# Reordering the seven weight operands in a piece of the down projection

## The chip, the cores and the metric

The kernel runs on one core of one Trainium2 chip. The metric is the device time of one launch in microseconds, the median of several runs. The core has a matrix engine (TensorE; the profile calls its matmuls PE and its weight loads PEld), a vector engine (DVE), a scalar engine (ACT), GpSimd (POOL, here used only to issue transfers) and SyncE (SP, the other issuer of transfers).

## The reference

One layer of a hybrid streaming encoder is run for 384 tokens: 256 frames of a new stream and 8 running streams of 16 frames. A mixer (causal pooling, and a Mamba-2 scan) comes first, then the part in which the change lies:

```python
x = x + rmsnorm(m, p['g_mix_post'])
hdn = jnp.square(jax.nn.relu(rmsnorm(x, p['g_mlp_pre']) @ p['w_up'])) @ p['w_down']
x = x + rmsnorm(hdn, p['g_mlp_post'])
```

w_up is 2048 x 8192, w_down 8192 x 2048, all in float32. The change touches only the order of the work in the product with w_down.

## The kernel before

**Split operands.** Every float32 product is made from two rounded parts of each operand, a high part h and the rest l, and three matmuls: h·h, h·l and l·h. For a weight tile of 128 x 1024 ACT writes the high part (wh) and DVE, when ACT is done, the rest (wl = w - wh). Both come from a pool of three buffers each (wpool, bufs=3), handed out in turn, so the split of one weight half can begin only when TensorE has done its last matmul with the half three before it. All weight halves of the program use these three buffers.

**The MLP stage.** The 384 tokens are three blocks of 128. `up(f)` computes 128 hidden columns: two weight halves with 24 matmuls of 384 columns each. `combine(p)` forms from two of those the left operands of the down projection: blocks of the hidden tile themselves (H11, H31, H22, H12, H32, H3) and sums of them (S1 to S4), by five DVE instructions, two ACT instructions and two DVE subtractions for the rests. After eight `up` calls a chunk c of 1024 hidden rows is ready, four pairs p = 0 to 3, and two pieces follow, `blocks(c, 0)` and `blocks(c, 1)`, with four `up` calls of the next chunk after each. There are 15 pieces; the last quarter of the output for the last chunk is done without them.

**A piece.** `blocks(c, sb)` takes 1024 hidden rows and 1024 output columns. The first two token blocks are multiplied as 2 x 2 blocks with seven products in place of eight (Strassen's scheme in Winograd's form); the third block is multiplied plainly, its sums staying in the PSUM banks A and B over all chunks. Four weight tiles of 128 x 2048 (w11, w12, w21, w22, one buffer each) are fetched over POOL's queue (L1291). From them come seven operands, each split in two halves u = 0, 1 of 1024 columns, the half u serving the pairs p = 2u and 2u+1:

| operand | weight | left operand and PSUM bank | products |
|---|---|---|---|
| a | W11 | H11 into X, H31 into A | 2 |
| b | W21 | H12 into Y, H32 into A | 2 |
| c | W11+W12 | S1 into Y | 1 |
| d | W11+W12+W22 | S2 into X | 1 |
| e | W12+W22 | H31 into B, S3 into X | 2 |
| f | W22 | S4 into Y, H3 into B | 2 |
| g | W21+W11+W12+W22 | H22 into X | 1 |

A product of a half is 2 pairs x 3 matmuls = 6 matmuls of 512 columns. A piece has 11 products, 2 halves of each, so 132 matmuls. X and Y are read out seven times a piece in all by `evict` (L1323): DVE adds or subtracts the bank into the accumulator `acc` in SBUF; in the first chunk ACT copies instead, where the accumulator's block is written for the first time. X and Y keep accumulating after a read-out, so the next matmul into the bank waits until it has been read.

The sums of weights are made by DVE (`add`, L1306, two instructions of 1024 columns each): t1 = w11+w12 and w12 += w22 at the head of the piece, w11 += w12 (L1347), and t1 = w21+w11 (L1355), which overwrites operand c with operand g.

**What sets the order.** TensorE's order is written out: `run` (L1310) holds each group of matmuls behind the one before. For DVE, ACT and POOL the program's order is a priority, not the order of execution: when the program is built, each engine's instructions are put in a row in which an instruction whose inputs are expected to be ready goes ahead of one that stands earlier in the program and is not ready. On the chip each engine then runs its row strictly in order. In the text a piece is told by the time since its first weight load, and `u` (as a unit of time) is the time of six matmuls of 512 columns.

Of the kernel before, what the change touches and what calls it, by code (L numbers as in the profile page):

```python
# [10 lines left out]
ALU = mybir.AluOpType  # L11
# [22 lines left out]
def build(ctx, tc, io):  # L34
# [175 lines left out]
    def in_units(i):  # L210
        return [win[i - 5, 0], win[i - 5, 1]]
# [131 lines left out]
    for b in range(3):  # L343
# [3 lines left out]
            out=dgl[:, b, :], in0=ident, scalar=y1, in1=dgh[:, b, :].bitcast(F32), op0=ALU.mult, op1=ALU.subtract  # L347
# [9 lines left out]
    with tc.tile_pool(name="phc", bufs=1, reuse_waits="tile") as pc, tc.tile_pool(name="phc2", bufs=2, reuse_waits="tile") as pc2:  # L357
# [185 lines left out]
    with tc.tile_pool(name="phd", bufs=2, reuse_waits="tile") as pd, tc.tile_pool(  # L543
        name="phd1", bufs=1, reuse_waits="tile"
# [4 lines left out]
        for i in range(3):  # L549
            b = pd1.tile([P, 24, 19], F32, name=f"cbuf{i}")  # L550
# [292 lines left out]
        for g in range(G + 1):  # L843
# [74 lines left out]
            S1 = D.p[1]  # L918
# [84 lines left out]
    with tc.tile_pool(name="phf", bufs=1, side="right", reuse_waits="tile") as pf, tc.tile_pool(  # L1003
        name="phf2", bufs=2, side="right", reuse_waits="tile"
# [32 lines left out]
        A, L = [], []  # L1037
# [48 lines left out]
        for nb in range(4):  # L1086
# [3 lines left out]
            o = [sstile(f"wo{nb}_{b}") for b in range(3)]  # L1090
# [148 lines left out]
    with ExitStack() as mlp:  # L1239
# [44 lines left out]
        H11, H31, H22, H12, H32, S3, H3, S1, S2, S4 = range(10)  # L1284

        def blocks(c, sb):
            nm = f"{c}_{sb}"
            w = {}
            for i, k in enumerate(("11", "12", "21", "22")):
                w[k] = pr.tile([P, 2048], F32, tag=f"w{k}", name=f"w{k}_{nm}")  # L1290
                gp.dma_start(w[k], io["w_dn"][c, sb, i])  # L1291
            X, Y = (psd.tile([P, 512], F32, tag=n, name=f"{n}{nm}") for n in ("X", "Y"))
            A, B = c3[2 * sb], c3[2 * sb + 1]
            lo_, hi_ = slice(0, 1024), slice(1024, 2048)
            both = (lo_, hi_)
            left, rght = blk(2 * sb), blk(2 * sb + 1)
            C11, C12, C21, C22 = acc[:, 1, left], acc[:, 1, rght], acc[:, 0, left], acc[:, 0, rght]

            def split(t, u, name):
                h = wpool.tile([P, 1024], F32R, tag="wh", name=f"wh_{name}{nm}_{u}")  # L1300
                l = wpool.tile([P, 1024], F32R, tag="wl", name=f"wl_{name}{nm}_{u}")
                s.activation(h, t[:, both[u]], AF.Copy)
                v.tensor_tensor(l, t[:, both[u]], h.bitcast(F32), ALU.subtract)
                return h, l

            def add(out, a, b):  # L1306
                for q in both:
                    v.tensor_tensor(out[:, q], a[:, q], b[:, q], ALU.add)

            def run(hl, seq):  # L1310
                with behind(last[0]):
                    for p, out, j, start in seq:
                        wh, wl = hl
                        h, l, _ = HB[4 * c + p]
                        q = slice(p % 2 * 512, p % 2 * 512 + 512)
                        t = slice(j * P, j * P + P)
                        o, vh, vl = pairs(out), woven(wh[:, q]), woven(wl[:, q])
                        start = start and p == 0
                        te.matmul(o, h[:, t], vh, start=start, stop=False, skip_group_check=True)  # L1319
                        te.matmul(o, h[:, t], vl, start=False, stop=False, skip_group_check=True)  # L1320
                        last[0] = te.matmul(o, l[:, t], vh, start=False, stop=False, skip_group_check=True)  # L1321

            def evict(dst, src, op=ALU.add, first=False):  # L1323
                if first and c == 0:
                    s.activation(dst, src, AF.Copy, scale=-1.0 if op == ALU.subtract else 1.0)
                    return
                v.tensor_tensor(dst, dst, src, op)

            t1 = pr.tile([P, 2048], F32, tag="e", name=f"e{nm}")
            add(t1, w["11"], w["12"])  # L1330
            add(w["12"], w["12"], w["22"])
            a0 = split(w["11"], 0, "a")
            run(a0, [(p, o, j, g) for o, j, g in ((X, H11, True), (A, H31, c == 0)) for p in (0, 1)])
            b0 = split(w["21"], 0, "b")
            run(b0, [(p, o, j, g) for o, j, g in ((Y, H12, True), (A, H32, False)) for p in (0, 1)])
            a1 = split(w["11"], 1, "a")
            b1 = split(w["21"], 1, "b")
            run(a1, [(2, X, H11, False)])
            run(b1, [(2, Y, H12, False)])
            run(a1, [(2, A, H31, False), (3, X, H11, False)])  # L1340
            evict(C11, X, first=True)
            run(b1, [(3, Y, H12, False)])
            evict(C11, Y)
            run(b1, [(2, A, H32, False)])
            run(a1, [(3, A, H31, False)])
            run(b1, [(3, A, H32, False)])
            add(w["11"], w["11"], w["12"])  # L1347

            def simple(t, name, out, j, start):
                for u in (0, 1):  # L1350
                    run(split(t, u, name), [(p, out, j, start) for p in (2 * u, 2 * u + 1)])

            simple(t1, "c", Y, S1, True)
            evict(C22, Y, first=True)
            add(t1, w["21"], w["11"])  # L1355
            simple(w["11"], "d", X, S2, False)
            evict(C12, X, ALU.subtract, first=True)
            e0, e1 = split(w["12"], 0, "e"), split(w["12"], 1, "e")
            run(e0, [(p, B, H31, c == 0) for p in (0, 1)])
            run(e1, [(p, B, H31, False) for p in (2, 3)])  # L1360
            run(e0, [(p, X, S3, False) for p in (0, 1)])
            run(e1, [(p, X, S3, False) for p in (2, 3)])
            evict(C22, X, ALU.subtract)
# [34 lines left out]
        with tc.tile_pool(name="phg", bufs=1, reuse_waits="tile") as pg, tc.tile_pool(  # L1398
            name="phg2", bufs=2, reuse_waits="tile"
# [42 lines left out]
            for nb in (2, 3):  # L1442
                o = [mmtile(f"wd{nb}_{b}") if nb == 2 else psd.tile([P, 512], F32, tag="XY"[b], name=f"wd{nb}_{b}") for b in range(2)]
# [22 lines left out]
                w = []  # L1466
                for kp in range(4):
# [3 lines left out]
                    f_, name = wfetch(io["w_tail"][1, kp], f"wt3_{kp}")  # L1471
# [133 lines left out]
```

## Time and profile before

| | us |
|---|---|
| median of 3 runs | 2651.95 (2651.3 to 2653.32) |
| the profiled execution | 2653.36 |
| its span | 2651.6 |
| PE busy in the span | 2619.0 |
| DVE busy in the span | 1779.1 |
| ACT busy in the span | 1301.5 |

A profiled execution is one run; its own time is 1.76 us above its span and 1.41 us above the median. In the rows below the first column of a timeline is the start in us from the beginning of the span, the second the duration. "[1.54 <-DVE wl_d L1303]" says that the engine stood idle for 1.54 us and that the DVE instruction of line 1303 that writes wl_d ended the wait. A tile's name is followed by its inputs: `X<-wl_d,hh` is a matmul, or its weight load, into the bank X with the rest of operand d.

### The profile page before, as it was taken

What the parts mean: (1) busy time and instruction counts of PE and PEld (TensorE: products, weight loads), DVE (VectorE), ACT (ScalarE), POOL (GpSimd) and SP (SyncE); (2) the same over time, 40 slices, a digit from 0 to 9 for tenths busy, and PEclk for the clock granted to TensorE, in tenths of its full rate; (3) what the DMA queues carried; (4) which work ended last, traced back from release to release, by engine and by line L of the source; (5) the groups of instructions that cost most, each with busy time, mean ns of one, the idle gap of its engine ahead of it and who ended that gap; (6) DMA issues with size and microseconds to landing.
All of it is one profiled execution on the core that took longest, in us unless ns stands there. A gap on an engine that the chain in (4) does not pass through costs nothing.

```text
span 2651.6 us, 40353 instructions
## 1 busy us (share of the span) xinstructions
PE 2619.0 (99%) x15999; PEld 2504.6 (94%) x15999; DVE 1779.1 (67%) x2383; ACT 1301.5 (49%) x1981; POOL 184.2 (7%) x261
## 2 busy tenths in 40 slices
PE   9999999999999999999999999999999999999998
PEld 8999999999999999999999988998989999999997
DVE  6676334788787888766444436667676767767677
ACT  5443235557566666645333335545454444444454
POOL 0000000011110111121000000000000000000000
PEclk9999999999999999999999999999999999999999
DMA  7444446566666676657555554533444444433342
GB/s 273 140 138 153 147 147 206 182 208 209 224 216 212 205 230 212 229 203 245 183 159 159 168 178 163 183 127 135 152 147 139 139 143 139 135 136 135 128 173 105
DMA packets 139421, 457.77 MB, mean 173 GB/s; under 512 B 17568, under 2 KB 44768, under 8 KB 125792
## 3 DMA queue, kind: packets, MB, share of 16 engines
q1 hardware_dynamic: 117552, 330.12, 38.1%
q0 software_dynamic: 21680, 125.07, 12.6%
q8 instruction: 126, 2.06, 0.3%
q14 instruction: 63, 0.52, 0.1%
HBM read 410.26 MB, written 44.86 MB: 172 GB/s over the span
## 4 chain that ended last, share of the span: by engine, by line
PE 92%; DVE 5%; ACT 2%; issue 1%; DMA 0%; DVEq 0%; POOL 0%; ACTq 0%; POOLq 0%
PE pj_up L100 6%; PE pj_up L99 6%; PE pj_up L101 6%; PE pj_x L99 4%; PE pj_x L101 4%; PE pj_x L100 4%; PE pj_z L101 3%; PE pj_z L99 3%; PE pj_sp L100 3%; PE pj_sp L101 3%; PE pj_sp L99 3%; PE pj_z L100 3%; PE X L1320 2%; PE pj_gb L99 2%; PE c L1321 2%; PE c L1319 2%
## 5 line engine op out<-in xcount | busy, mean ns | idle before, releaser
L101 PE MATMUL pj_up<-x1h,wl_up 128*128 128x384 f32 (+1 forms) x1024 | 334.2, 326 | 0.0
L99 PE MATMUL pj_up<-x1h,wh_up 128*128 128x384 f32 (+1 forms) x1024 | 333.9, 326 | 0.0
L100 PE MATMUL pj_up<-x1l,wh_up 128*128 128x384 f32 (+1 forms) x1024 | 333.7, 326 | 0.0
L99 PE MATMUL pj_x<-xgh,wh_x 128*128 128x384 f32 x768 | 252.0, 328 | 0.0
L101 PE MATMUL pj_x<-xgh,wl_x 128*128 128x384 f32 x768 | 250.6, 326 | 0.9 <-DVE wl_x L72 0.9
L100 PE MATMUL pj_x<-xgl,wh_x 128*128 128x384 f32 x768 | 250.4, 326 | 0.0
L71 ACT ACTIVATE wh_up<-w_up 128x1024 fp32r<-128x1024 f32 x126 | 133.0, 1056 | 187.2 <-PE pj_up L100 148.0
L72 DVE TENSOR_TENSOR wl_up<-w_up,wh_up 128x1024 fp32r<-128x1024 f32 x126 | 152.7, 1221 | 100.1 <-ACT wh_up L71 99.0
L101 PEld LDWEIGHTS pj_up<-x1h,wl_up 128*128 128x128 f32 x1024 | 193.5, 189 | 0.9
L100 PEld LDWEIGHTS pj_up<-x1l,wh_up 128*128 128x128 f32 x1024 | 193.5, 189 | 0.4
L99 PEld LDWEIGHTS pj_up<-x1h,wh_up 128*128 128x128 f32 x1024 | 193.5, 189 | 0.4
L99 PE MATMUL pj_sp<-abh,wh_sp 128*128 128x384 f32 x512 | 166.9, 326 | 0.0
L100 PE MATMUL pj_sp<-abl,wh_sp 128*128 128x384 f32 x512 | 166.9, 326 | 0.0
L101 PE MATMUL pj_sp<-abh,wl_sp 128*128 128x384 f32 x512 | 166.9, 326 | 0.0
L101 PE MATMUL pj_z<-xgh,wl_z 128*128 128x384 f32 x512 | 166.9, 326 | 0.0
L100 PE MATMUL pj_z<-xgl,wh_z 128*128 128x384 f32 x512 | 166.9, 326 | 0.0
L99 PE MATMUL pj_z<-xgh,wh_z 128*128 128x384 f32 x512 | 166.9, 326 | 0.0
L72 DVE TENSOR_TENSOR wl_sp<-w_sp,wh_sp 128x1024 fp32r<-128x1024 f32 x64 | 78.3, 1223 | 116.6 <-ACT wh_sp L71 116.6
L71 ACT ACTIVATE wh_x<-w_x 128x1024 fp32r<-128x1024 f32 x96 | 101.0, 1052 | 107.0 <-PE pj_z L100 53.0
L72 DVE TENSOR_TENSOR wl_x<-w_x,wh_x 128x1024 fp32r<-128x1024 f32 x96 | 117.2, 1221 | 52.2 <-ACT wh_x L71 52.2
L71 ACT ACTIVATE wh_sp<-w_sp 128x1024 fp32r<-128x1024 f32 x64 | 67.7, 1058 | 166.4 <-PE pj_sp L100 158.3
L99 PEld LDWEIGHTS pj_x<-xgh,wh_x 128*128 128x128 f32 x768 | 145.1, 189 | 2.6 <-issue 0.4
(449 smaller groups left out, 7122.5 us busy)
## 6 DMA issues: line engine op xcount, KB each, us to landing
w_up<-w_up SPq DMA_DIRECT2D x128, 512.0 KB, 3.5
w<-w_dn POOLq DMA_DIRECT2D x60, 1024.0 KB, 6.7
w_x<-w_in SPq DMA_DIRECT2D x96, 512.0 KB, 3.8
w_z<-w_in SPq DMA_DIRECT2D x64, 512.0 KB, 3.5
w_sp<-w_ssd SPq DMA_DIRECT2D x64, 512.0 KB, 3.5
w_ga<-w_ga SPq DMA_DIRECT2D x32, 512.0 KB, 3.4
w_pp<-w_pp SPq DMA_DIRECT2D x32, 512.0 KB, 3.5
hs<-ssm POOLq DMA_DIRECT2D x16, 1024.0 KB, 6.6
```

Of the source, the lines that this page charges most:

```text
L71: cut[0] = s.activation(h, w, AF.Copy)
L72: cut[1] = v.tensor_tensor(l, w, h.bitcast(F32), ALU.subtract)
L99: te.matmul(out, wh, xh, start=first, stop=False, **how)
L100: te.matmul(out, wh, xl, start=False, stop=False, **how)
L101: return te.matmul(out, wl, xh, start=False, stop=last, **how)
L1319: te.matmul(o, h[:, t], vh, start=start, stop=False, skip_group_check=True)
L1320: te.matmul(o, h[:, t], vl, start=False, stop=False, skip_group_check=True)
L1321: last[0] = te.matmul(o, l[:, t], vh, start=False, stop=False, skip_group_check=True)
```

## The change

The order in a piece before is a and b interleaved, then c, d, e, f, g. After it is a and c interleaved, then f, d, e, b, g, so that operands with two products (a, f, e, b) and with one (c, d, g) alternate. The sum t1 = w21+w11 moves from behind operand c to behind operand e. Operand f is done like e, in the new `double`: both halves are split first, then the first product runs over both halves, then the second; before, f's first half did both products before its second half came. The bank Y holds c and then f's product on top, read out as C22 and C12, and is begun anew for b. The numbers of matmuls, splits, sums, read-outs and transfers are unchanged.

```diff
-            a0 = split(w["11"], 0, "a")
+            def simple(t, name, out, j):
+                for u in (0, 1):
+                    run(split(t, u, name), [(p, out, j, False) for p in (2 * u, 2 * u + 1)])
+
+            def double(t, name, first, second):
+                e = [split(t, u, name) for u in (0, 1)]
+                for out, j, start in (first, second):
+                    for u in (0, 1):
+                        run(e[u], [(p, out, j, start) for p in (2 * u, 2 * u + 1)])
+
+            a0, c0 = split(w["11"], 0, "a"), split(t1, 0, "c")
             run(a0, [(p, o, j, g) for o, j, g in ((X, H11, True), (A, H31, c == 0)) for p in (0, 1)])
-            b0 = split(w["21"], 0, "b")
-            run(b0, [(p, o, j, g) for o, j, g in ((Y, H12, True), (A, H32, False)) for p in (0, 1)])
-            a1 = split(w["11"], 1, "a")
-            b1 = split(w["21"], 1, "b")
-            run(a1, [(2, X, H11, False)])
-            run(b1, [(2, Y, H12, False)])
-            run(a1, [(2, A, H31, False), (3, X, H11, False)])
+            run(c0, [(p, Y, S1, True) for p in (0, 1)])
+            a1, c1 = split(w["11"], 1, "a"), split(t1, 1, "c")
+            run(a1, [(2, X, H11, False), (2, A, H31, False)])
+            run(c1, [(2, Y, S1, False)])
+            run(a1, [(3, X, H11, False), (3, A, H31, False)])
             evict(C11, X, first=True)
-            run(b1, [(3, Y, H12, False)])
+            run(c1, [(3, Y, S1, False)])
+            evict(C22, Y, first=True)
+            add(w["11"], w["11"], w["12"])
+            double(w["22"], "f", (B, H3, c == 0), (Y, S4, False))
+            evict(C12, Y, first=True)
+            simple(w["11"], "d", X, S2)
+            evict(C12, X, ALU.subtract)
+            double(w["12"], "e", (B, H31, False), (X, S3, False))
+            evict(C22, X, ALU.subtract)
+            add(t1, w["21"], w["11"])
+            double(w["21"], "b", (Y, H12, True), (A, H32, False))
             evict(C11, Y)
-            run(b1, [(2, A, H32, False)])
-            run(a1, [(3, A, H31, False)])
-            run(b1, [(3, A, H32, False)])
-            add(w["11"], w["11"], w["12"])
...
-            simple(t1, "c", Y, S1, True)
-            evict(C22, Y, first=True)
-            add(t1, w["21"], w["11"])
-            simple(w["11"], "d", X, S2, False)
-            evict(C12, X, ALU.subtract, first=True)
-            e0, e1 = split(w["12"], 0, "e"), split(w["12"], 1, "e")
-            run(e0, [(p, B, H31, c == 0) for p in (0, 1)])
-            run(e1, [(p, B, H31, False) for p in (2, 3)])
-            run(e0, [(p, X, S3, False) for p in (0, 1)])
-            run(e1, [(p, X, S3, False) for p in (2, 3)])
-            evict(C22, X, ALU.subtract)
-            f0, f1 = split(w["22"], 0, "f"), split(w["22"], 1, "f")
-            run(f0, [(p, o, j, False) for o, j in ((Y, S4), (B, H3)) for p in (0, 1)])
-            run(f1, [(p, o, j, False) for o, j in ((Y, S4), (B, H3)) for p in (2, 3)])
-            evict(C12, Y)
-            simple(t1, "g", X, H22, False)
+            simple(t1, "g", X, H22)
             evict(C21, X, first=True)
```

More of the change, by code (lines that the diff above doesn't have):

```diff
@@ L1341, in blocks @@
-            evict(C11, X, first=True)
-            run(b1, [(3, Y, H12, False)])
-            evict(C11, Y)
-            run(b1, [(2, A, H32, False)])
-            run(a1, [(3, A, H31, False)])
-            run(b1, [(3, A, H32, False)])
-            add(w["11"], w["11"], w["12"])
-            def simple(t, name, out, j, start):
-                for u in (0, 1):
-                    run(split(t, u, name), [(p, out, j, start) for p in (2 * u, 2 * u + 1)])
-            simple(t1, "c", Y, S1, True)
```

## The prediction

> **What bounds the kernel now.** I read the page first, then the waits of TensorE's weight loads, then the busy time of single pieces, then one piece instruction by instruction.
>
> ```profile
> span 2651.6 us, 40353 instructions
> PE 2619.0 (99%) x15999; PEld 2504.6 (94%) x15999; DVE 1779.1 (67%) x2383; ACT 1301.5 (49%) x1981; POOL 184.2 (7%) x261
> ```
>
> TensorE is busy for 99% of the span, so an order of operands can only win or lose the gaps between its matmuls. The waits of the weight loads (line, releaser: us in total, times, longest) name the gaps in the pieces:
>
> ```profile
> PEld X L1320 <- DVE wl_d L1303: 22.0, 15, 1.5
> PEld Y L1320 <- DVE wl_c L1303: 6.7, 15, 0.7
> ...
> PEld Y L1319 <- issue: 4.8, 13, 0.4
> PEld Y L1320 <- DVE wl_b L1303: 4.6, 8, 0.6
> ```
>
> Together 38.1 us in 51 gaps, once per piece for operands c and d. The weight loads of one piece (a `blocks(c, 0)` piece, which comes straight after a `combine`) show what a gap costs:
>
> ```profile
> 2085.15 0.19 PEld L1319 LDWEIGHTS X<-wh_a,hh 128*128 128x128 f32 x1
> ...
> 2087.47 0.19 PEld L1321 LDWEIGHTS c<-wh_a,hl 128*128 128x128 f32 x1
> ...
> 2091.69 0.19 PEld L1320 LDWEIGHTS Y<-wl_b,hh 128*128 128x128 f32 x1 [0.58 <-DVE wl_b L1303]
> ...
> 2102.03 0.19 PEld L1320 LDWEIGHTS X<-wl_d,hh 128*128 128x128 f32 x1 [1.54 <-DVE wl_d L1303]
> 2102.14 0.19 PEld L1321 LDWEIGHTS X<-wh_d,hl 128*128 128x128 f32 x1
> ...
> 2103.01 0.19 PEld L1319 LDWEIGHTS c<-wh_e,hh 128*128 128x128 f32 x1
> ...
> 2108.18 0.19 PEld L1319 LDWEIGHTS Y<-wh_f,hh 128*128 128x128 f32 x1
> ...
> 2115.95 0.19 PEld L99 LDWEIGHTS pj_up<-x1h,wh_up 128*128 128x128 f32 x1
> ```
>
> From 2103.01 to 2108.18 24 loads run without a gap, 0.2155 us each; six of them, one product of one half, are u = 1.293 us. A load that had to wait is followed by the next after 0.11 us, so 0.10 us of every delay is caught back. An idle of 0.03 us (0.2155 - 0.189) is no gap. So 38.1 us of idle cost 38.1 - 51 x 0.13 = 31 us. The piece itself agrees: 2115.95 - 2085.15 = 30.80 us against 132 x 0.2155 = 28.45 us, a loss of 2.35. The busy table of such a piece and of one of the other parity (no `combine` just before) gives the second:
>
> ```profile
> 2085.15:2115.95 30.80, 29.45 (x133) 24.60 (x133) 25.44 (x29) 16.77 (x18) 2.11 (x4) 1.00 0.38 137
> 2147.24:2177.60 30.36, 29.17 (x133) 24.68 (x133) 24.12 (x27) 15.65 (x17) 2.11 (x4) 1.00 0.38 139
> ```
>
> 30.36 - 28.45 = 1.91 lost there. (Columns: stretch, length, busy us of PE, PEld, DVE, ACT, POOL, granted clock, transfers.) DVE is busy for 25.4 of 30.8 us: not the bound by its sum, but the one that is late. Its row of that piece:
>
> ```profile
> 2086.43 1.23 DVE L1303 TENSOR_TENSOR wl_a<-w,wh_a 128x1024 fp32r<-128x1024 f32 x1 [2.67 <-ACT wh_a L1302]
> ...
> 2089.08 1.22 DVE L1308 TENSOR_TENSOR w<-w,w 128x1024 f32<-128x1024 f32 x1
> ...
> 2090.42 1.22 DVE L1303 TENSOR_TENSOR wl_b<-w,wh_b 128x1024 fp32r<-128x1024 f32 x1
> 2091.55 0.82 DVE L1276 TENSOR_TENSOR hl<-S,hh 128x640 fp32r<-128x640 f32 x1
> 2092.29 1.22 DVE L1303 TENSOR_TENSOR wl_c<-e,wh_c 128x1024 fp32r<-128x1024 f32 x1
> ...
> 2099.03 1.22 DVE L1308 TENSOR_TENSOR e<-w,w 128x1024 f32<-128x1024 f32 x1
> 2100.17 0.68 DVE L1327 TENSOR_TENSOR acc<-acc,Y 128x512 f32<-128x512 f32 x1
> 2100.77 1.22 DVE L1303 TENSOR_TENSOR wl_d<-w,wh_d 128x1024 fp32r<-128x1024 f32 x1
> ...
> 2112.28 1.22 DVE L1303 TENSOR_TENSOR wl_g<-e,wh_g 128x1024 fp32r<-128x1024 f32 x1 [0.93 <-ACT wh_g L1302]
> 2113.42 0.68 DVE L1327 TENSOR_TENSOR acc<-acc,Y 128x512 f32<-128x512 f32 x1
> 2114.02 1.22 DVE L1308 TENSOR_TENSOR e<-w,w 128x1024 f32<-128x1024 f32 x1
> 2115.15 1.22 DVE L72 TENSOR_TENSOR wl_up<-w_up,wh_up 128x1024 fp32r<-128x1024 f32 x1
> ```
>
> Two readings carry the rest. First, DVE's slots: a split or a sum takes 1.14 us of the row (2099.03 to 2100.17), the second subtraction of `combine` 0.74, a read-out 0.60. Second, sums fill gaps: w11's sum (2089.08) stands ahead of the split of b, and t1's second half (2099.03) with the read-out behind it ahead of the split of d, though d's buffer was free by then. That cost the 1.54 us at wl_d.
>
> **A split's own chain** needs two rows of ACT.
>
> ```profile
> 2088.10 1.06 ACT L1302 ACTIVATE wh_b<-w 128x1024 fp32r<-128x1024 f32 x1
> ...
> 2111.19 1.06 ACT L1302 ACTIVATE wh_g<-e 128x1024 fp32r<-128x1024 f32 x1 [1.53 <-PE c L1321]
> ```
>
> wh_b begins 0.63 us after the last load with a's first half, whose buffer it takes (2087.47 to 2088.10). DVE follows ACT's start by 1.09 (2111.19 to 2112.28); the load that uses wl comes 1.22 + 0.04 after DVE's start (2100.77 to 2102.03). So 2.98 us from the last load of the half three before to the first load with wl, which is the second load of the new half. If N is where a half is due and F where its buffer is freed, in u, its slack is (N - F)u + 0.43 - 2.98: at 2u it is 0.04 us, at 1.5u it is -0.61.
>
> **The change, step by step.** The counts of matmuls, splits, sums, read-outs and transfers stay, so nothing is added to any engine. What moves is due times. Old order: c's second half has 1.5u (its buffer was a's second), d, e and the next `up` 2u, f, g and c's first 3u to 4u. New order, F to N: c1 2u to 4u, f0 3 to 6, f1 5.5 to 7, d0 6 to 10, d1 9 to 11, e0 10 to 12, e1 11 to 13, b0 12 to 16, b1 15 to 17, g0 16 to 20, g1 19 to 21, up 20 to 22. One half (f1) again has 1.5u, and seven have 2u, that is nothing to spare if DVE is not idle at that moment. The old gaps (31 us) go. The new ones, with the rule that DVE takes what is ready, earlier program line first:
>
> *c1.* It takes the buffer and DVE slot that b1 had: start 2090.42 - 2085.15 = 5.27, ready at 6.53. b1 was due at 4.5u + 0.22 = 6.04, c1 at 4u + 0.22 = 5.39: late by 1.14, net 1.04. In the other seven pieces the slot is earlier:
>
> ```profile
> 2147.24 0.19 PEld L1319 LDWEIGHTS X<-wh_a,hh 128*128 128x128 f32 x1
> ...
> 2151.34 1.22 DVE L1303 TENSOR_TENSOR wl_b<-w,wh_b 128x1024 fp32r<-128x1024 f32 x1
> ```
>
> 4.10, ready at 5.36: just in time, 0.
>
> *f1.* After `combine` DVE has from 5.27: c1 to 6.40, hl to 7.14, f0 to 8.27, read-out of X to 8.87, then t1's second half, the only thing ready since Y's read-out must wait for c's last matmuls, to 10.01, Y's read-out to 10.61, f1 ready at 11.87. Due at 7u + 0.22 + 1.04 = 10.31: late 1.56, net 1.46. In the other pieces c1 begins at 4.10, f0 about 5.5, t1 to 7.75, both read-outs to 8.95, f1 ready 10.21, due 9.27: net 0.84. The lower bound is the buffer alone: 0.61, net 0.5.
>
> *d1 and e.* DVE is idle before d1, so d1 is in time. With D the delay so far, d1's DVE slot begins at 9u - 0.22 + 1.72 + D = 13.15 + D and ends 14.28 + D; Y's read-out (ready since 13.35 + D) goes next, e0 from 14.88 is ready at 16.14 + D against 15.75 + D: net 0.29. When e0's slot ends at 16.02 + D, X's read-out after d has been ready for 0.08 us and precedes e1: late 0.54, net 0.44. With 0.08 us the other way, e1 goes first and this term is 0.
>
> *g1 and the next up.* g1's slot ends at 19u - 0.22 + 1.72 + 1.13 = 27.2 + D, the first `up` half could begin at 27.4 + D. Into 0.2 us slips a sum of the next piece (as at 2114.02, where one more unit of lead hid it): the `up` half is late by 1.14 - 0.2 - 0.1 = 0.83, net 0.73; 0 if nothing is ready or DVE took it earlier. For that w12 must have landed:
>
> ```profile
> 2104.55 0.53 POOL L1291 DMA_DIRECT2D w<-w_dn  x1 [1.74 <-DVE wl_e L1303]
> ...
> w<-w_dn POOLq DMA_DIRECT2D x60, 1024.0 KB, 6.7
> ```
>
> It is issued 0.3 us after e's second split, in the new order some 20 us into the piece, and lands 6.7 later, about 27: it may be ready or not by a hair. The other transfers on POOL's queue cost nothing: w22's goes out about 12 us earlier than now, w11's stays, w21's moves from 15.7 to about 25.5, with some 35 us until its next reader. POOL has nothing else in this stage, and SP's w_up loads keep their buffers. The seven read-outs have at least 2u = 2.59 us before the next matmul into their bank and need 0.63 + 0.68 + 0.1; delays of up to 1.1 us stay hidden.
>
> *Sum.* After a `combine` 1.04 + 1.46 + 0.29 + 0.44 + 0.73 = 3.96, else 0.84 + 0.29 + 0.44 + 0.73 = 2.30. 8 x 3.96 + 7 x 2.30 = 47.8; less 0.7 for the last piece, which no next sum follows, and 2.5 for the two pieces of the first chunk, whose first read-outs are ACT's: 44.6. Minus the old 31: +13.6 us on the profiled execution (2653.36, whose span is 2651.6), 2667.0; on the median of 2651.95, 1.4 lower, 2665.5.
>
> [...] In both pieces quoted the granted clock is 1.00, with three or four gaps of up to 1.54 us. [...]
>
> **Rivals.** *1, the intended gain.* The sums move out of the crowd: if DVE splits c1, f1 and e ahead of the sum and read-outs, only f1's buffer chain is left, 15 x 0.5 = 7.5 us; 2651.95 - 31 + 7.5 = 2628. It decides at f1 and c1: a sum there must not stand ahead of the split. For it speaks that t1's first half can now be made before the piece (it needs only c0's split at -2.6); against it that w11's sum stands ahead of b1 at 2089.08 today, and c1 takes that place. *2, the ties fall well.* e1 goes before the read-out (-0.44 x 15 = -6.6) or the next sum does not slip in ahead of `up` (-0.73 x 14 = -10.2): one of them gives 2655 to 2659, both 2649, no change. *3, the clock halves* after the longer gaps. A slow stretch at the start of the program has this price:
>
> ```profile
> 8.54 1.49 PE L309 MATMUL pj_p<-xgh,wh_e 128*128 128x384 f32 x4
> 9.82 0.99 PE L309 MATMUL pj_p<-xgl,wh_e 128*128 128x384 f32 x4
> ...
> 11.30 0.33 PE L99 MATMUL pj_p<-xgh,wh_e 128*128 128x384 f32 x1
> 11.46 0.33 PE L100 MATMUL pj_p<-xgl,wh_e 128*128 128x384 f32 x1
> ```
>
> Four matmuls took 1.28 us, 0.32 each, then 0.16: half speed until about 10 us, begun with the first at 4.2, so some 2.8 us lost; in 15 pieces 42 us, with the forecast's gaps 2707.
>
> **How the numbers follow.** About 0.2%, 5.3 us, is what a measurement here can tell from no change. The forecast, 0.40, 2665.5. One tie well, 0.23, of which the greater part is above 2657.3. Both ties, 0.13, no change. Rival 1, whole or in part (only one kind of piece keeps its sum out of the way), 0.14, faster. Clock, 0.02. Other small mixtures, 0.08. Slower 0.65, same 0.21, faster 0.14. The range, 2645 to 2671, holds the forecast, both ties and 5 us above it, for a sum that catches both g1 and `up`; rival 1 and the clock are left out. The likeliest case's own range is 2660 to 2671.
>
> **What would show it.** wl_d at X gone from the waits; in its place wl_c at Y (1.1 us, 8 times), wl_f at B (0.9 and 1.5, 15 times), wl_e at B (0.4 to 0.5) and wl_up at pj_up (0.8). Pieces of about 32 us after a `combine` and 30.5 otherwise, against 30.8 and 30.4. Gaps of wl_f at 0.6 and none at wl_c would show rival 1, a clock under 1.00 in the pieces rival 3. Wrong would be the row that I give DVE: it is set when the program is built, and ties of 0.1 us decide two of the five terms.

## The result and the profile after

The changed kernel takes 2685.0 us (median of 4 runs, 2683.66 to 2685.55) beside 2652.53 us for the kernel before on the same chip (4 runs, 2651.3 to 2653.32): 1.0122 times as long, 95% interval 1.0105 to 1.014. It is slower, as forecast, but by 32.5 us where 13.6 were forecast, and above the range given. The profiled execution took 2683.66 us with a span of 2681.9, 30.3 us more than that of before.

Head of the page, the row of the w_dn transfers, and the first four waits of the weight loads, all of the kernel after:

```profile
span 2681.9 us, 40347 instructions
PE 2624.3 (98%) x15999; PEld 2509.8 (94%) x15999; DVE 1780.1 (66%) x2383; ACT 1302.4 (49%) x1981; POOL 184.1 (7%) x261
...
w<-w_dn POOLq DMA_DIRECT2D x60, 1024.0 KB, 5.1
```

```profile
PEld pj_up L101 <- DVE wl_up L72: 26.3, 14, 3.0
PEld c L1320 <- DVE wl_f L1303: 19.0, 15, 1.6
PEld Y L1320 <- DVE wl_c L1303: 9.8, 8, 1.2
PEld c L1320 <- DVE wl_e L1303: 7.0, 15, 0.5
```

The counts of work are the same, and DVE's busy time changed by 1 us. The 22.0 us of wl_d are gone. The waits that the prediction listed have come, at wl_c 8 times, at wl_f 15 times, at wl_e 15 times and at wl_up 14 times; but the last is the largest, 26.3 us with single waits of 3.0, where 0.8 each was forecast.

The busy table (stretch, length, busy us of PE, PEld, DVE, ACT, POOL, granted clock, transfers) of a piece after a `combine`, of one without, and of two stretches of 3 us at the start of the `up` calls that follow the second:

```profile
2095.22:2126.56 31.34, 29.24 (x134) 24.68 (x134) 23.41 (x27) 16.89 (x18) 2.11 (x4) 1.00 0.39 134
2158.67:2188.45 29.78, 28.97 (x134) 24.76 (x133) 21.90 (x25) 15.65 (x17) 2.11 (x4) 1.00 0.40 141
2189.00:2192.00 3.00, 0.34 (x2) 0.19 (x2) 3.00 (x5) 2.73 (x4) 0.00 (x0) 1.00 0.00 0
2192.00:2195.00 3.00, 3.00 (x11) 3.00 (x11) 3.00 (x4) 0.00 (x0) 0.00 (x0) 0.53 0.58 186
```

The pieces lost 2.89 and 1.33 us against 28.45; before it was 2.36 and 1.91. All 15 together lose 31.1 us, as much as before. That is a coincidence, since not one of the gaps is the same. What grew is the time between the pieces, in which TensorE stood idle for 2.66 of 3 us and then ran for about 3.4 us at a granted clock of one half. Measured from the first load of `up` to the first load of the next piece:

| us | before | after |
|---|---|---|
| 15 pieces, loss in all | 31.1 | 31.1 |
| `up` calls after `blocks(c, 0)`, 7 times | 31.29 each | 32.11 each |
| `up` calls after `blocks(c, 1)`, 7 times | 31.28 each | 34.18 (2), 35.86 (4), 35.25 (the first) |

That is 7 x 0.82 = 5.7 and 247.05 - 218.96 = 28.1, together +33.8 us. The stage with the pieces began 3.5 us earlier in this execution than in that of before (1711.65 against 1715.11), which leaves the +30.3 of the profiled execution. That start is no effect of the order: another profile of the same kernel has it at 1713.52, and one of the order before (the run with its sum held back, below) at 1713.42.

What DVE did in the stretch of 2.66 us (start, duration, line, out <- in), and ACT's row for the half that is waited for:

```profile
2186.07 1.22 DVE L1303 TENSOR_TENSOR wl_g<-e,wh_g 128x1024 fp32r<-128x1024 f32 x1 [1.62 <-ACT wh_g L1302]
2187.33 1.22 DVE L1308 TENSOR_TENSOR e<-w,w 128x1024 f32<-128x1024 f32 x1
2188.47 0.82 DVE L1268 TENSOR_TENSOR hl<-R,hh 128x640 fp32r<-128x640 f32 x1
2189.20 0.68 DVE L1327 TENSOR_TENSOR acc<-acc,X 128x512 f32<-128x512 f32 x1
2189.80 0.82 DVE L1276 TENSOR_TENSOR hl<-S,hh 128x640 fp32r<-128x640 f32 x1
2190.54 2.35 DVE L72 TENSOR_TENSOR wl_up<-w_up,wh_up 128x1024 fp32r<-128x1024 f32 x2
```

```profile
2186.27 1.06 ACT L71 ACTIVATE wh_up<-w_up 128x1024 fp32r<-128x1024 f32 x1 [0.24 <-PE c L1321]
```

wh_up began at 2186.27; by the chain of the prediction wl_up could start 1.09 later, at 2187.36. A sum of the next piece began 0.03 us earlier, as forecast. But behind the sum three more instructions went first: the two subtractions of `combine(4c+4)`, which stands ahead of this `up` in the program, and a read-out. wl_up began at 2190.54, 3.2 us late. In the kernel before, at the same place, wl_up went ahead of them:

```profile
2175.67 1.22 DVE L1308 TENSOR_TENSOR e<-w,w 128x1024 f32<-128x1024 f32 x1
2176.80 1.22 DVE L72 TENSOR_TENSOR wl_up<-w_up,wh_up 128x1024 fp32r<-128x1024 f32 x1
2177.94 0.81 DVE L1268 TENSOR_TENSOR hl<-R,hh 128x640 fp32r<-128x640 f32 x1
```

In the `up` loop after `blocks(c, 0)` no `combine` stands, and in the kernel after only the sum slips in:

```profile
2124.18 1.23 DVE L1303 TENSOR_TENSOR wl_g<-e,wh_g 128x1024 fp32r<-128x1024 f32 x1 [1.62 <-ACT wh_g L1302]
2125.43 1.22 DVE L1308 TENSOR_TENSOR e<-w,w 128x1024 f32<-128x1024 f32 x1
2126.58 1.22 DVE L72 TENSOR_TENSOR wl_up<-w_up,wh_up 128x1024 fp32r<-128x1024 f32 x1
```

### The profile page after: what moved, and what is told of

It is laid out like the page before. It is cut to its first block, busy times and chain, and to the rows that moved or that the text cites. A ratio compares the mean times of both kernels' runs of the same rounds, so it can differ in the third digit from the quotient of the medians.

```text
span 2681.9 us, 40347 instructions
## 1 busy us (share of the span) xinstructions
PE 2624.3 (98%) x15999; PEld 2509.8 (94%) x15999; DVE 1780.1 (66%) x2383; ACT 1302.4 (49%) x1981; POOL 184.1 (7%) x261
## 3 DMA queue, kind: packets, MB, share of 16 engines
q1 hardware_dynamic: 117552, 330.12, 38.1%
q8 instruction: 126, 2.06, 0.3%
## 4 chain that ended last, share of the span: by engine, by line
PE 86%; DVE 8%; ACT 2%; issue 2%; DMA 1%; SPq 0%; DVEq 0%; POOL 0%; ACTq 0%; POOLq 0%
PE pj_up L101 6%; PE pj_up L100 6%; PE pj_up L99 6%; PE pj_x L99 4%; PE pj_x L101 4%; PE pj_x L100 4%; PE pj_z L100 3%; PE pj_sp L99 3%; PE pj_sp L101 3%; PE pj_z L101 3%; PE pj_sp L100 3%; PE pj_z L99 3%; PE pj_gb L99 2%; PE pj_gb L100 2%; PE pj_gb L101 2%
## 5 line engine op out<-in xcount | busy, mean ns | idle before, releaser
L101 PEld LDWEIGHTS pj_up<-x1h,wl_up 128*128 128x128 f32 x1024 | 196.2, 192 | 26.3 <-DVE wl_up L72 26.3
```

Of the source, the lines that this page charges most:

```text
L101: return te.matmul(out, wl, xh, start=False, stop=last, **how)
```

## Experiments: the time between the pieces

**The combine behind the up.** If the two subtractions are what is late, tracing the `combine` behind its `up` leaves only the sum's 1.07 us. The gaps named in what follows are the time between two loads beyond the usual 0.2155.

```diff
             for f in range(4, 8):
+                up(8 * c + 8 + f)
                 if f < 6:
                     combine(4 * c + f, c == NC - 2)
-                up(8 * c + 8 + f)
```

> The new order, with combine(4c+4) and combine(4c+5) traced after the up call that they stood ahead of, so that their two subtractions no longer go ahead of the split of the first up half after blocks(c, 1). Theory (the long gap after blocks(c, 1) is the sum of the next piece, 1.14 us, plus two subtractions of 0.74 and a read-out of 0.60 on DVE ahead of that split, and the clock falls because the gap is long): the gap of 3.14 us between the two loads becomes about 1.07, as after blocks(c, 0), 7 x 2 = 14 us; the stretches at 0.32 us a load vanish, 5 x 1.7 = 8.5 us; 2685 becomes about 2662. Rival A (the next piece's sum or its transfer alone makes the gap): the gap stays at 3.1, 2685. Rival B (the clock falls from the many gaps of a piece, not from the long one): the gap shrinks, the slow stretches stay, about 2670.

Measured: 2664.52 us (2662.78 to 2666.03), 1.005 times before (1.0034 to 1.0067). The wait at `up`, and DVE's row after a `blocks(c, 1)`:

```profile
PEld pj_up L101 <- DVE wl_up L72: 12.4, 14, 0.9
```

```profile
2179.15 1.23 DVE L1308 TENSOR_TENSOR e<-w,w 128x1024 f32<-128x1024 f32 x1
2180.30 1.22 DVE L72 TENSOR_TENSOR wl_up<-w_up,wh_up 128x1024 fp32r<-128x1024 f32 x1
```

All 14 gaps are now 1.07 us, all stretches 32.11, and no load runs at half speed. The pieces did not change. So some 20 of the 32.5 us come from `combine` standing ahead of `up`: by the rows 13.9 as idle time (6 x 2.07 + 1.47 in the first chunk) and 8.4 as clock (5 x 1.68). Of these 22.3 us the span shows 20.9, since in this run the stage began 0.8 us later and the last piece lost 0.6 us more.

**The head sums behind the up.** The sum is the first link of that chain: without it wl_up would be the first thing ready.

```diff
-            add(t1, w["11"], w["12"])
-            add(w["12"], w["12"], w["22"])
+            with behind(mark[0]):
+                add(t1, w["11"], w["12"])
+                add(w["12"], w["12"], w["22"])
...
             for f in range(4):
                 up(8 * c + 8 + f)
+                if f == 0:
+                    mark[0] = cut[1]
```

`behind` holds what stands inside it behind the instruction that it is given. Here that is `cut[1]`, DVE's second split of the first `up` after a piece. In the diffs below, `cuts["f", 1]` is DVE's split of f's second half, and the others are named likewise.

> The new order, with the sums at the head of a piece (t1 and w12) queued on DVE behind the splits of the first up call after the piece before, so that none slips in ahead of the first up half. Theory (the sum is the pusher: without it DVE is free before the combine's subtractions are ready): both kinds of gap after a piece go, 0.9 us after blocks(c, 0) and 3.0 after blocks(c, 1), 7 x 0.9 + 6 x 3.0 + 2.4 = 27 us, and with them the slow stretches, 8.5 us; about 2650. Rival (the subtractions have the earlier program line and go first anyway): only 1.1 us goes at each of the 14 places; a gap of about 2 us stays after blocks(c, 1); 2669 with the slow stretches left in part.

Measured: 2651.1 us (2649.98 to 2654.15), 1.0001 times before (0.9991 to 1.001). DVE's row at the same place:

```profile
2176.11 1.22 DVE L72 TENSOR_TENSOR wl_up<-w_up,wh_up 128x1024 fp32r<-128x1024 f32 x1
2177.25 0.82 DVE L1269 TENSOR_TENSOR hl<-R,hh 128x640 fp32r<-128x640 f32 x1
```

wl_up goes ahead of the subtractions although these still stand earlier in the program: it is ready first. The stretches between pieces are 31.25 us, as before the change, and the wait at `up` is gone. The pieces still lose 2.88 and 1.33. The sums of 1.14 us, each let in a few hundredths of a us ahead of a split of `up`, carried the whole loss of 32.5 us.

## Experiments: inside the pieces

**t1's second half behind f1.** The prediction put f1's delay down to this sum, which DVE takes while it waits for Y.

```diff
-            add(t1, w["21"], w["11"])
+            v.tensor_tensor(t1[:, lo_], w["21"][:, lo_], w["11"][:, lo_], ALU.add)
+            with behind(cuts["f", 1]):
+                v.tensor_tensor(t1[:, hi_], w["21"][:, hi_], w["11"][:, hi_], ALU.add)
```

> The new order, with the second half of t1 = w21+w11 queued on DVE behind the split of f's second half. Theory (that sum, 1.14 us, stands ahead of the split): the gap at wl_f falls from 1.56 us after a combine and 1.15 otherwise to about 0.7, what f1's buffer alone costs, 8 x 0.85 + 7 x 0.45 = 10 us; the rest stays; about 2675. Rival (the buffer chain or the read-outs set f1's time): the gap at wl_f stays within 0.1 us, 2685.

Measured: 2671.18 us (2670.4 to 2671.43), 1.0073 times before (1.0058 to 1.0088). DVE's row after a `combine`, in the kernel after and in this one:

```profile
2102.36 1.22 DVE L1303 TENSOR_TENSOR wl_f<-w,wh_f 128x1024 fp32r<-128x1024 f32 x1
2103.50 0.68 DVE L1327 TENSOR_TENSOR acc<-acc,X 128x512 f32<-128x512 f32 x1
2104.09 1.22 DVE L1308 TENSOR_TENSOR e<-w,w 128x1024 f32<-128x1024 f32 x1
2105.23 0.68 DVE L1327 TENSOR_TENSOR acc<-acc,Y 128x512 f32<-128x512 f32 x1
2105.82 1.22 DVE L1303 TENSOR_TENSOR wl_f<-w,wh_f 128x1024 fp32r<-128x1024 f32 x1
```

```profile
2099.16 1.22 DVE L1305 TENSOR_TENSOR wl_f<-w,wh_f 128x1024 fp32r<-128x1024 f32 x1
2100.30 0.68 DVE L1329 TENSOR_TENSOR acc<-acc,X 128x512 f32<-128x512 f32 x1
2101.24 0.69 DVE L1329 TENSOR_TENSOR acc<-acc,Y 128x512 f32<-128x512 f32 x1 [0.27 <-PE Y L1323]
2101.85 1.22 DVE L1305 TENSOR_TENSOR wl_f<-w,wh_f 128x1024 fp32r<-128x1024 f32 x1
```

f1's gap falls from 1.55 and 1.15 to 0.78 in both kinds of piece, and the losses to 2.10 and 0.97. The floor of 0.61 for the buffer alone was nearly right: ACT began f1's high part at 2100.60 in this run, so f1 could have been split from 2101.69, and the read-out of Y, which had waited for PE, took the other 0.16. The gaps of 3.14 us after `blocks(c, 1)` are unchanged, but only one of the seven was followed by half speed, against five in the kernel after. The gain of 12.3 us in the span (2681.9 to 2669.6) is 6.3 us from the pieces (6 x 0.79 + 6 x 0.36, less 0.6 in the last one) and 6.7 from the clock, less 0.8 for a later start of the stage. The clock's part was not expected; the section on it below takes it up.

**w11's second half behind c1.** The same for the gap at c1.

```diff
-            add(w["11"], w["11"], w["12"])
+            v.tensor_tensor(w["11"][:, lo_], w["11"][:, lo_], w["12"][:, lo_], ALU.add)
+            with behind(cuts["c", 1]):
+                v.tensor_tensor(w["11"][:, hi_], w["11"][:, hi_], w["12"][:, hi_], ALU.add)
```

> The kernel after, with the second half of w11 + w12 (operand d's sum) held on VectorE's queue until c's second split is out. In after, c1 waits 1.19 us after a combine because this sum and the combine's small subtractions go ahead of its split. Theory one, the queue as a whole is what is short until f's second half: the 1.19 us at c1 goes, but the sum then stands ahead of f's first split, f0 and f1 come later by about as much, and in the pieces without a gap at c1 the f1 gap grows from 1.15 to about 1.8 us; the sum over a pair of pieces stays or grows: 2685 to 2690 us. Theory two, each sum is a cost of its own slot and the work behind it has slack: c1's gap goes in eight pieces and nothing comes back, 2685 - 8 x 1.1 = 2676 us. The up stretches keep their gaps of 1.07 and 3.14 us between loads; how many of the seven long ones are followed by loads at half speed is open (five in after, one in the run with t1's half held back).

Measured: 2678.7 us (2677.18 to 2682.37), 1.0105 times before (1.0088 to 1.0122). The waits:

```profile
PEld c L1322 <- DVE wl_f L1305: 25.4, 23, 1.9
...
PEld Y L1322 <- DVE wl_c L1305: 1.7, 8, 0.2
```

c1's gap goes from 1.19 to 0.18, and f pays for it: f0 is now late by 0.52 after a `combine`, and f1's gap in the other pieces grows from 1.15 to 1.82, as theory one had it. A pair of pieces loses 1.82 + 2.01 = 3.83 instead of 4.22, so 7 x 0.39 = 2.7 us stay. The span is 4.1 us shorter: 2.7, and 3 x 1.7 since two of the seven gaps were followed by half speed in place of five, less 3.8 for a later start of the stage. So of the 1.01 us gained at c1 some 0.4 stayed in a pair of pieces and the rest was passed on: DVE's queue up to f1 is short as a whole. The time lies below the expected 2685 to 2690 us. They had left the clock as it was, and with its 5 us the time would be near their lower end.

**The sum held back in the kernel before.** The old order lost 1.52 us at d to the second half of the same t1. Here it is traced behind e's splits.

```diff
             e0, e1 = split(w["12"], 0, "e"), split(w["12"], 1, "e")
+            with behind(cuts["e", 1]):
+                v.tensor_tensor(t1[:, hi_], w["21"][:, hi_], w["11"][:, hi_], ALU.add)
```

> The order before, with the second half of t1 = w21+w11 queued on DVE behind the split of e's second half. Theory (in the order before, too, that sum ahead of a split makes the largest gap): the 1.52 us at wl_d go, some 0.3 and 0.5 come back at wl_e, since the read-outs of Y and X then stand ahead of e's splits; net 0.65 x 15 = 10 us, 2652.5 becomes about 2642. Rival (DVE is behind by the sum of its work, so the gap only moves to e): 2652.

Measured: 2641.71 us (2640.63 to 2642.95), 0.9962 times before (0.9949 to 0.9975). Its first wait in the pieces:

```profile
PEld c L1322 <- DVE wl_e L1305: 13.2, 28, 0.7
```

The 22.0 us at wl_d are gone, 13.2 at wl_e appear (0.22 and 0.66 per piece), and the pieces lose 1.62 and 1.17. The old order had the same illness as the new, a sum that stands in DVE's queue long before it is needed, and half of the cure stays.

## Experiments: the parts together

**Both held-back sums that helped**, the head sums behind `up` and t1's half behind f1 (the two diffs above).

> The kernel after with both edits that were tried alone: the head sums of the next piece behind the first up's splits, and the second half of t1 = w21 + w11 behind f1's split. If the two causes are independent, the gain of the first (2685.0 - 2651.1 = 33.9 us) and that of the pieces in the second (f1's gap 1.55 to 0.78 and 1.15 to 0.78, measured 0.79 and 0.36 per piece over 13 pieces, about 7.5 us) add: 2651.1 - 7.5 = 2643.6 us, faster than before by 0.3%. If the head sums, once moved, were what hid or fed the other gap, it would stay at 2651 or fall by more than 10 us.

Measured: 2645.55 us (2642.89 to 2646.21), 0.9973 times before (0.9963 to 0.9982): the gains add, within 2 us. The pieces lose 2.10 and 0.97, the stretches between them are 31.25.

**All five places**: these two, w11's half behind c1, Y's second read-out behind e0's split, and f half by half, which gives f1 2.5u on its buffer in place of 1.5u. Y is now read out after X, so X's read-out is the one that writes C12 for the first time. The diff shows the last two of the five. ("The second edit" in the expectation is w11's.)

```diff
-            double(w["22"], "f", (B, H3, c == 0), (Y, S4, False))
-            evict(C12, Y, first=True)
+            f0, f1 = split(w["22"], 0, "f"), split(w["22"], 1, "f")
+            for u, hl in ((0, f0), (1, f1)):
+                run(hl, [(p, o, j, g) for o, j, g in ((B, H3, c == 0), (Y, S4, False)) for p in (2 * u, 2 * u + 1)])
             simple(w["11"], "d", X, S2)
-            evict(C12, X, ALU.subtract)
+            evict(C12, X, ALU.subtract, first=True)
             double(w["12"], "e", (B, H31, False), (X, S3, False))
+            with behind(cuts["e", 0]):
+                evict(C12, Y)
```

> After with its order of operands kept and five places of VectorE's queue put right: the head sums behind the first up's splits, the second halves of w11 + w12 and of t1 = w21 + w11 behind c1's and f1's splits, Y's second read-out behind e0's split, and f run half by half (f0's four products, then f1's), so that f1 falls due 1.29 us later. The run of the second edit alone left 0.18 us at c1, 0.52 us at f0 and 1.14 us at f1 after a combine, and 1.82 us at f1 in the other pieces. If every gap of the pieces is a matter of that queue, the gaps at f1 and e0 (0.41) go with the other edits, c1's 0.2 and f0's 0.5 stay in half of the pieces, a piece loses 0.0 to 0.6 us where before lost 1.9 and 2.4, and the kernel takes 2651.1 - 31 + 15 x 0.3 = about 2625 us, 1% faster than before. If something else holds TensorE in the pieces (the wh and wl tiles it must give back, a transfer of w), the gaps reappear there and the time stays above 2638 us.

Measured: 2626.4 us (2624.47 to 2627.74), 0.9907 times before (0.989 to 0.9923). Two pieces and what is left of the waits in the pieces:

```profile
2072.39:2101.44 29.05, 28.90 (x134) 24.68 (x133) 23.55 (x27) 16.77 (x18) 2.11 (x4) 1.00 0.43 145
2132.70:2161.13 28.43, 28.43 (x133) 24.92 (x133) 22.31 (x25) 15.65 (x17) 2.11 (x4) 1.00 0.44 148
```

```profile
PEld c L1323 <- DVE wl_f L1306: 5.1, 9, 0.7
...
PEld Y L1322 <- DVE acc L1330: 1.8, 7, 0.3
PEld Y L1323 <- DVE wl_c L1306: 1.7, 8, 0.2
```

A piece without a `combine` has no gap left (28.43 us for 132 loads), one after a `combine` loses 0.60. With the same order of operands the kernel is 59 us faster than the kernel after and 25 us faster than before. Apart from the last piece, no buffer and no transfer held TensorE: the gaps were DVE's queue, and the one buffer bound, f1's, went with the change to half by half. The last piece lost 0.6 us more than the others of its kind to a transfer: ACT's scaling of g_mlp_post stands ahead of f's second split there and waits for g_mlp_post to land. Whether the old order would come as low with all its sums placed by hand was not tried.

## Experiments: the clock

**The changed kernel once more.** Five of seven gaps of the same kind were followed by half speed in the kernel after, one in the run with t1's half held back.

> The changed kernel itself, unedited, profiled once more. If the loads at half speed follow from the program, five of the seven gaps of 3.1 us are followed by them again, at the same pieces, and the span is 2682 us. If they depend on when the gap falls in something that runs on its own, other pieces or another number show them, 1.7 us each.

Measured: 2686.5 us, span 2684.7. Four of seven, and at other places: after the pieces that began at 2029.75, 2158.83, 2415.30 and 2544.38; in the first profile at 1774.16, 1902.17, 2158.67, 2287.75 and 2544.24. The first loads at half speed (they took 0.29 to 0.32 us in place of 0.19) began at 2063.48, 2193.21, 2449.20 and 2578.93. They lie 129.73, 255.99 and 129.73 us apart: 38, 75 and 38 times 3.413 to 3.414. The same holds in the first profile (1806.51, 1936.27, 2192.08, 2321.81, 2577.82: 38.0, 74.9, 38.0 and 75.0 times). So in both profiles the clock was lowered at the marks of one grid of 3.413 us, which ran on through the 38 and 75 intervals between, and where a gap fell on the grid differed from run to run. The granted clock shows the marks directly when the busy table is cut at them: it is 0.50 for exactly one interval. First the interval with most of a gap and the one behind it from the second profile, then the same from the first, where the clock stayed up:

```profile
2575.52:2578.92 3.40, 1.40 (x8) 1.40 (x9) 3.40 (x5) 1.92 (x3) 0.00 (x0) 1.00 0.07 19
2578.93:2582.34 3.41, 3.41 (x12) 3.41 (x12) 3.41 (x5) 0.00 (x0) 0.00 (x0) 0.50 0.81 279
```

```profile
2062.47:2065.88 3.41, 1.48 (x9) 1.48 (x10) 3.41 (x5) 1.85 (x3) 0.00 (x0) 1.00 0.16 25
2065.89:2069.30 3.41, 3.41 (x23) 3.41 (x22) 3.41 (x5) 1.06 (x1) 0.00 (x0) 1.00 0.90 280
```

TensorE was idle for 2.00 us of the one interval and for 1.93 of the other. In the run with t1's half held back six of the gaps came every 126.26 us, that is 36.99 intervals, so that all six fell on nearly the same place of the grid; none was followed by half speed. Sorted by the largest part of a gap's idle time between two marks, the 28 gaps of four profiles (two of the kernel after, two of the runs above) fall apart at about 2 us: 2.00 and more was followed by half speed 12 times of 12, 1.93 and less 0 times of 16. (The expectations below have 2.03 and 1.99, from marks placed by the loads.)

**A shorter and a longer gap** test that. In the first the `combine`'s second subtraction is traced behind the `up`, in the second both subtractions are done twice, writing the same values again.

```diff
+            for _ in range(again):
+                v.tensor_tensor(l[:, raws], R[:, P:], h[:, raws].bitcast(F32), ALU.subtract)
+                v.tensor_tensor(l[:, rest], S, h[:, rest].bitcast(F32), ALU.subtract)
...
-                    combine(4 * c + f, c == NC - 2)
+                    combine(4 * c + f, c == NC - 2, 1 if f == 4 else 0)
```

> After, with the second subtraction of the combine before the first up (the one of S) traced after that up: the gap ahead of wl_up loses one slot of 0.74 us, so TensorE idles for 2.65 - 0.74 = 1.91 us in six of the stretches after blocks(c, 1), and 1.3 in the first. In the four profiles so far the half-speed stretches begin at multiples of 3.413 us from one another, and a gap was followed by one when at least 2.03 us of its idle time fell between two such marks (12 of 12), not when the largest part was 1.99 us or less (16 of 16). By that reading no gap is followed by half speed any more, whatever its position: 0 of 7, and the time is 2685.0 - 7 x 0.74 - 5 x 1.7 = 2671 us. If a gap's length only sets a chance, which fell on 12 of 28 so far, two or three of seven would still show it: 2675 us.

> After, with the two subtractions of the combine before the first up done twice (the same values are written again), so that the idle time of TensorE in the six long gaps is 2.65 + 1.47 = 4.12 us, and 3.53 in the first. However such a gap lies on a grid of 3.413 us, one part is at least 2.06 us. By the reading of the grid every one of the six is followed by loads at half speed, and the first one mostly: 6 or 7 of 7, at 1.7 us or a little more each, 2685.0 + 7 x 1.47 + 2 x 1.7 = 2698.7 us. If it is a chance of some 4 in 10 for a gap, three of seven would show it: 2692 us.

Measured: 2675.51 us (2675.3 to 2676.29) with one gap of seven followed by half speed, and 2700.82 us (2698.57 to 2704.17) with all seven (both counts from the profiled execution). The waits at `up` of the two:

```profile
PEld pj_up L101 <- DVE wl_up L72: 21.1, 14, 2.2
```

```profile
PEld pj_up L101 <- DVE wl_up L72: 36.6, 14, 4.4
```

The longer gap did what the grid says and excludes the plain chance, which gave 2692. In three of its seven stretches the clock stayed at 0.50 for two intervals, 6.83 us, which cost 2.7 to 3.0 us in place of 1.5 to 1.7. In these three the gap ran on for 0.68 to 1.34 us into the first interval at half speed; in the other four it ran on for 0.34 us at most. An interval that was idle as a whole cost no more by itself: of two such, one was followed by two intervals and one by a single one. The shorter gap came out between: none was expected and one was seen, the single one whose 1.92 us of idle lay wholly between two marks; the others had 1.74 or less on one side. With the 1.93 above that left the clock alone, the edge is not as sharp as my expectation had it, and lies somewhere from 1.9 to 2.0 us. Its time is 4 us above the 2671 expected: 1.7 are that one stretch, and the stage with the pieces began 3.7 us later in this execution than in the first profile of the kernel after.

## Why the prediction was right in sign and too small in size

- *The old gaps go; the counts stay.* Right: no wait at wl_d, the same matmuls, DVE within 1 us. (38.1 - 51 x 0.13 is 31.5 rather than the 31 put down for the old gaps; the pieces measured 31.1.)
- *c1.* 1.14 late, 8 times: measured 1.19, 8 times. Right.
- *f1.* 1.56 after a `combine`: measured 1.55. 0.94 in the others: measured 1.15, as t1's half went ahead of f0 (2164.11 against 2165.24) and a small subtraction of `combine` (one of four, not of five as in the description of the kernel) into the wait for Y. The held-back sum showed the cause and the floor.
- *d1 and e.* No wait at d1, and 0.41 to 0.46 at e0 where 0.39 was forecast. The tie at e1 fell the other way: both splits of e went ahead of X's read-out, the term of 0.44 was 0, 6.6 us in all.

```profile
2112.66 2.35 DVE L1303 TENSOR_TENSOR wl_e<-w,wh_e 128x1024 fp32r<-128x1024 f32 x2
2114.93 0.68 DVE L1327 TENSOR_TENSOR acc<-acc,X 128x512 f32<-128x512 f32 x1
```

- *g1 and the next up.* **This is the step that failed.** It gave 0.73 for all 14 places. For the seven after `blocks(c, 0)` that was right (0.82). For the seven after `blocks(c, 1)` it was 2.9 (34.18 - 31.29), in the first chunk 2.3, where no read-out by DVE stands. The step asked which *sum* could slip into the 0.2 us, found one, and stopped. It did not ask what becomes ready while that sum runs and stands ahead of `up` in the program: two subtractions of `combine` and a read-out, 2.07 us more in all. In the kernel before wl_up had gone ahead of them because it was ready first; the sum took that lead away. Moving the `combine` alone, and the sum alone, showed both links.
- *The clock.* Rival 3 had a chance of 0.02 and was priced at the gaps of the pieces, of up to 1.56 us; those left the clock alone but for one pair in the last piece of another execution (last section). The 3.1 us gaps were not in the forecast, so their price was not either: 5 x 1.7 = 8.4 us. The chance of 0.02 was the author's estimate, from pieces at a granted clock of 1.00 with gaps of up to 1.54 us; in the profiled execution 2.65 us of idle were enough in four of six places, and 2.06 in the first chunk.
- *Transfers.* Right that the loads of w_dn cost nothing. Their landing became shorter (6.7 to 5.1 us), as the four loads of a piece no longer go out in a bunch (5.0, 2.9 and 5.2 us apart in the piece shown, 1.5, 2.3 and 5.4 in the kernel before): there a load issued while another was on its way took 7.0 us (median of 45), a lone one 5.1. So w12 was not ready by a hair: in the piece shown it landed some 3.6 us ahead of the sum (2183.7 against 2187.33). POOL's queue does have one thing more at the end of the stage, the transfer of g_mlp_post. ACT waits for it in the last piece, in the new order ahead of f1's split. In the first profile of the kernel after this cost nothing beyond f1's usual gap, in the second 1.0 us, and the half speed behind it 1.7 more.

The sum, on the profiled execution: +13.6 forecast. The pieces came out 3.4 us lower than forecast (the tie at e1 -6.6, f1, e0 and c1 the rest), the first loads of `up` cost 25.4 in place of 10.2, the clock added 8.4: 13.6 - 3.4 + 15.2 + 8.4 = 33.8, less 3.5 for the earlier start of the stage: the measured 30.3. Three of the five terms were about right, e1's was nothing, and the last was three to four times too small in half of its places. The sign did not hang on that: with the last term as forecast the sum would have been 13.6 - 3.4 = +10.2. The intended gain was not out of reach: the kernel with all five places put right takes 2626.4, near rival 1's 2628. That the two are so close is partly luck, since rival 1 kept f1's buffer chain (7.5 us), which half by half took away, and had nothing for the 0.6 us that a piece after a `combine` still loses.

## What to carry to other kernels

An order of operands is only as good as the queue of the engine that prepares them: before costing a new order, write out that queue around each split, and for each slot that something takes by being ready early, ask what else becomes ready while it runs. Work that is due late (a sum for the next piece, a read-out) is best held explicitly behind the splits that are due now; here that, together with f done half by half, was worth 59 us of 2685 with the order of operands unchanged; how much of it is f's was not measured. In this kernel an idle stretch of TensorE of 2 us or more could cost clock as well, 1.5 to 1.7 us for each interval at half speed, and single gaps of 1 us (the 14 of 1.07 us with the `combine` behind the `up`) cost their length alone.

## What the runs showed of the hardware that was not expected

In these runs the granted clock fell to one half after an idle time that was clearly shorter than the 3.41 us for which it then stayed down. For the 42 long gaps of six profiles, 2.00 us or more of idle between two marks of the 3.413 us grid were followed by it 19 times of 19 (12 in the four profiles, 7 with the longer gap), 1.89 to 1.93 us once of three, and 1.80 us or less never. For gaps of 2.65 us of idle the place on the grid decided, which differs from run to run.

The profiles allow a wider count, since the granted clock fixes the grid in each of them. The twelve profiles here hold 9287 intervals at full clock that lie wholly within a span. All 36 of them with 2.05 us or more of idle were followed by half speed, all 9246 with 1.89 us or less were not, and of the five between, those with 1.92, 1.94 and 2.00 us were and those with 1.93 and 2.01 were not. So the edge is not exact, or the idle times read from the profiles are not exact enough to show it. An interval at half speed was followed by another when TensorE was idle for 0.68 us or more of it (16 times of 16), and by full clock at 0.45 us or less (27 of 27).

It need not be one gap: in the second profile of the changed kernel the last piece had two, with a single load between them, 1.94 us of idle in one interval, and then ran at half speed too, from 2623.30, 13 intervals after 2578.93. The first of the two is the wait for ACT, which in turn had waited for g_mlp_post:

```profile
2618.75 1.91 ACT L1400 ACTIVATE gpo<-gpo 128x2048 f32<-128x2048 f32 x1 [2.61 <-DMA gpo<-g_mlp_post]
```

```profile
2621.66 0.19 PEld L1319 LDWEIGHTS c<-wh_f,hh 128*128 128x128 f32 x1 [1.57 <-ACT wh_f L1302]
2622.92 0.19 PEld L1320 LDWEIGHTS c<-wl_f,hh 128*128 128x128 f32 x1 [1.07 <-DVE wl_f L1303]
...
2623.24 0.27 PEld L1319 LDWEIGHTS c<-wh_f,hh 128*128 128x128 f32 x1
2623.60 0.34 PEld L1320 LDWEIGHTS c<-wl_f,hh 128*128 128x128 f32 x1
```

In the two profiles of the changed kernel the starts of the half-speed stretches lie multiples of 3.413 to 3.414 us apart, and in the twelve an interval that was idle for 60% of its length (2.05 of 3.41 us) was followed by half speed like an empty one. That the share of an interval counts, and not the length of a gap by itself, fits the 42 long gaps of six profiles, two of them made to test it, and the intervals of all twelve; what sets the share, and other forms of work than these matmuls, were not tried.
